# A second attention layer with its steps in another order, and weight halves made by converting and accumulating transfers

## The chip, the cores and the metric

The kernel runs on one core of a Trainium2 chip. Five engines run their own instruction queues: TensorE (PE, with its weight loads shown apart as PEld), VectorE (DVE), ScalarE (ACT), GpSimd (POOL) and SyncE (SP), which here only issues transfers. The metric is the time of one execution on the device in microseconds, as the median of several runs.

## The reference

A trunk of four residual layers over 256 tokens of width 1024 in float32, and a last RMSNorm. Layers 0 and 3 mix tokens with NSA attention, layer 1 with MoBA attention, layer 2 with a gated convolution; a SwiGLU feed-forward part (FFN) follows in each. The change works in layer 1:

```python
q, k, v = jnp.split(h @ w_in, 3, axis=-1)          # 16 heads of 64
n_blk = -(-S_ // MOBA_BLOCK)                       # 256 tokens are one block
...
n_sel = min(MOBA_TOPK, n_blk - 1)                  # 0: no past block to select
...
m_own = jnp.broadcast_to(own_pos[None, :] <= tq[:, None], (B_, H, Qc, MOBA_BLOCK))
s_own = jnp.einsum('bhqd,bhkd->bhqk', qc, k_own)
if n_sel == 0:
    p = masked_softmax(s_own, m_own)
    return jnp.einsum('bhqk,bhkd->bhqd', p.astype(v_own.dtype), v_own)
...
return o @ w_out
```

With 256 tokens and blocks of 256 this is causal attention of 16 heads, between two projections.

## The kernel before

**Weights.** A float32 product is made of three products of float32r halves, high×high, high×low and low×high. All weights come from one stream of 402 *parts* of 128x1024 float32 (512 KB), `in_w`. `load_part` (L115, SP) brings a part into a `raw` tile, `split_part` rounds it to `whi` (L176, `HI` names the engine) and takes `wlo` = raw − whi (L180, `LO` names the engine: "v" is DVE, "p" POOL in four pieces). `take` hands a part to the matmuls and makes `split_part` run for the next ones, so that five are under way. The pools hold six `raw`, five `whi` and five `wlo` tiles. `split_part` already has a branch for the letter "d" in `LO`; no table uses it before. In it a POOL transfer converts the part straight into a `raw` tile that serves as the high half, ACT writes its negative into `wlo`, and a second POOL transfer from the same place in memory is accumulated onto `wlo`. Nothing is left for DVE then, and that `raw` tile stays taken until PE has used it.

**The layer.** `MOBA_ORDER` lists its steps. V projects four parts for half of the values (L602 to L604, 128x512 matmuls); k and q project one part for one pair of heads, 24 matmuls of 128x256 (L206 to L208, with `at` as the other operand; DVE takes the result out of PSUM in L589); s makes a pair's scores (L692 to L694), then `softmax`: a masked reduction on DVE (L619), four exponentials on ACT (L622), a reciprocal `rc` on DVE (L624), and four multiplications of `pr` by it (L626, by the letters of `MOBA_BY`, POOL before). T transposes a pair's `pr` on PE (L704 to L707), P multiplies with the values (L206 to L208 with `pt`). The out projection (`moba_out`, L226 and L230) starts in between. There are eight pairs, 32 parts (103 to 134 of the stream, the last eight `moba_out`). In the FFN before it, POOL also sums squares (`ssq`, L293), and `rstd` (L307) follows at the layer's start.

A scheduler puts the instructions of each engine in a queue of their own by its estimate; waits between engines are semaphores. An engine's queue is taken strictly in order, POOL's transfers among its other instructions.

Of the kernel before, what the change touches and what calls it, by code (L numbers as in the profile page):

```python
# [9 lines left out]
F32 = mybir.dt.float32  # L10
F32R = mybir.dt.float32r
AF = mybir.ActivationFunctionType
OP = mybir.AluOpType
# [3 lines left out]
P = 128  # L17
D = 1024
S = 256
KT = D // P  # L20
NT = S // P
DFF = 2816
FT = DFF // P
DH = 64
# [3 lines left out]
PART = 8  # L28
# [8 lines left out]
ROW_BUFS = 7  # L37
PT_BUFS = 5
PS_BUFS = {"A": 4, "B": 3, "C": 1}
NSA_ORDER = ("A G q K0 F q F K2 F F g E q C K1 q q s q c s t T V D s K3 T q P s T P s q T T s P c P s T t P s "  # L40
             "P T T P P").split()
MOBA_ORDER = ("V k k q q k s V s T q q k s s P k T k q T P q P T P s q q T k s k T s s T P P T P P").split()
LO = {"nsa_out": "p", "moba_out": "vp", "A": "p", "F": "v"}
HI = {"moba_out": "v", "moba_q": "ava"}
OUT_BANKS = "AAAB"
CMP_BANK = "B"
GELU = "vector"
# [5 lines left out]
RUN = 2 * PART  # L53
LAG = 4
PROJ_BANKS = "AABB"
NSA_BY = ["p"] * 8
MOBA_BY = ["p"] * 8
OWN = "vava"
CONE = "vector"
NPAIR = 8  # L60
NCMP = 15
# [3 lines left out]
class Kernel:  # L65
    def __init__(self, ctx, tc, ap):
        self.tc, self.nc, self.ap = tc, tc.nc, ap
        self.operands = ctx.enter_context(tc.tile_pool(name="operands", bufs=2))
        self.const = ctx.enter_context(tc.tile_pool(name="const", bufs=1))
        self.wp = ctx.enter_context(tc.tile_pool(name="wp", bufs=3))  # L70
        self.work = ctx.enter_context(tc.tile_pool(name="work", bufs=2))
        self.ps = ctx.enter_context(tc.tile_pool(name="ps", bufs=2, space=PSUM))
        self.pos = 0
        self.raw = {}
        self.parts = {}
        self.jobs = []
        self.latest = []
        self.nblk = ap["w"].shape[0]
        self.names = [step for step, name, _, c in stream()
                      for _ in range(len(c) // P * (FT if name == "ffn_w_down" else 4 if step == "F" else KT))][::PART]  # L80
        self.seq, q = [], 0
        while q < self.nblk:
            if self.names[q] == "fast":
                self.seq += [(q, w) for w in FAST] + [(q + x, None) for x in range(4, KT)]
                q += KT
            else:
                self.seq.append((q, None))
                q += 1
        self.when = [0]
        for _, what in self.seq:  # L90
            self.when.append(self.when[-1] + (1 if what else 2))
        self.n = 0
# [54 lines left out]
    def split_part(self, x):  # L147
        nc = self.nc
        q, what = self.seq[x]
        if what:  # L150
            self.fast_part(x)
            return
        lo_eng, hi_eng = (e.get(self.names[q], d) for e, d in ((LO, "v"), (HI, "a")))
        lo_eng, hi_eng = (e[q % len(e)] if q >= 4 else d for e, d in ((lo_eng, "v"), (hi_eng, "a")))
        if lo_eng == "d":
            hi = self.wp.tile([P, PART * P], F32R, tag="raw", name=f"raw{q}", bufs=RAW_BUFS)
            lo = self.operands.tile([P, PART * P], F32R, tag="wlo", name=f"wlo{q}", bufs=W_BUFS)
            nc.gpsimd.dma_start(hi, self.ap["w"][q])
            nc.scalar.activation(lo, hi.bitcast(F32), AF.Identity, scale=-1.0)
            nc.gpsimd.dma_start(lo, self.ap["w"][q], accum_op=OP.add)  # L160
            self.parts[x] = (hi, lo)
            return
        if q not in self.raw:
            self.load_part(q)
        src = self.raw.pop(q)
        hi = self.operands.tile([P, PART * P], F32R, tag="whi", name=f"whi{q}", bufs=W_BUFS)
        lo = self.operands.tile([P, PART * P], F32R, tag="wlo", name=f"wlo{q}", bufs=W_BUFS)
        eng = {"p": nc.gpsimd, "v": nc.vector}[lo_eng]
        copy = {"a": nc.scalar.copy, "v": nc.vector.tensor_copy, "d": None}[hi_eng]
        n = PART * P // (2 if q < 4 else 1)  # L170
        if hi_eng == "d":
            nc.gpsimd.dma_start(hi, self.ap["w"][q])
        for o in range(0, PART * P, n):
            c = slice(o, o + n)
            if copy:
                copy(hi[:, c], src[:, c])  # L176
            m = n // (PIECES if eng is nc.gpsimd else 1)
            for b in range(o, o + n, m):
                d = slice(b, b + m)
                eng.tensor_tensor(out=lo[:, d], in0=src[:, d], in1=hi[:, d].bitcast(F32), op=OP.subtract)  # L180
        self.parts[x] = (hi, lo)
# [552 lines left out]


    def nsa(self, j, norm):
        nc, at = self.nc, self.begin(norm)
        mm = nc.tensor.matmul
        self.new_keys()
        w2 = self.sb([P, 2, 2, P], "w2", bufs=1)  # L740
# [8 lines left out]
        for a in range(2):  # L749
            nc.gpsimd.tensor_copy(xs[a][:, :, :, 16], pos[:, a, None, 8:].to_broadcast([P, 4, 8]))  # L750

        def put_raw(a, gp):
            def put(p):
                f = self.scaled(p)
                for i in range(2):
                    src = f[i * DH:(i + 1) * DH].rearrange("p (c r i) -> p i r c", i=2, r=8)
                    dst = xs[a][:, 2 * gp + i, :, :16]
                    nc.vector.tensor_copy(dst[:DH], src[:, 0])
                    nc.scalar.copy(dst[DH:], src[:, 1])
                if gp:  # L760
                    windows(a)
            return put

        def windows(a):
            for hf in range(2):
                for r in range(0, 8, 4):
                    x = self.ff([P, 2, S]).rearrange("p i s -> p (i s)").rearrange("p (r i g c) -> p r i g c", r=4, i=2, g=4)
                    src = xs[a][:, :, r:r + 4, hf:hf + 16].rearrange("p g r c -> p r g c")
                    nc.scalar.copy(x[:, :, 0], src)
                    nc.vector.tensor_tensor(out=x[:, :, 1], in0=src, in1=x[:, :, 0].bitcast(F32), op=OP.subtract)  # L770
                    if hf == 0:
                        src = pos[:, a, r:r + 4, None].to_broadcast([P, 4, 4])
                        nc.scalar.copy(x[:, :, 0, :, 15], src)
                        nc.vector.tensor_tensor(out=x[:, :, 1, :, 15], in0=src, in1=x[:, :, 0, :, 15].bitcast(F32),
                                                op=OP.subtract)
                    xw[a].append(x.rearrange("p r i g c -> p r (i g c)"))
# [103 lines left out]
        def compress_values(_):  # L880
# [4 lines left out]
            for g in range(4):  # L885
                rep = self.row().rearrange("p (i a c) -> p i a c", i=2, c=16)
                c = slice(DH + g * 16, DH + g * 16 + 16)
# [12 lines left out]
            for r in range(4):  # L900
                y = self.ff([P, 4 * P])
                on = self.rsel[:, r:r + 1]
                if OWN[r] == "a":
                    nc.scalar.activation(y, x, AF.Identity, scale=on)
                else:
                    {"v": nc.vector, "p": nc.gpsimd}[OWN[r]].tensor_scalar(y, x, on, None, op0=OP.mult)
                vc.append(y.rearrange("p (g c) -> p g c", g=4))

        ptc = self.sb([P, 4, S], "ptc", F32R, bufs=1)
# [45 lines left out]
        v = [[], []]  # L955
# [16 lines left out]
        def scores(p):  # L972
# [10 lines left out]
            for i in range(2):  # L983
                cols = [(s0[:, i, b], slice(b * P, (b + 1) * P)) for b in range(2)]
                cols += [(s1[i][:, b], slice((1 + b) * S, (2 + b) * S)) for b in range(2)]
                h = 2 * p + i
                g = [gates[:, t, 16 * (b + 1) + h:16 * (b + 1) + h + 1] for t in range(2) for b in range(2)]
                prs[p].append(self.softmax(cols, g, NSA_BY[p]))

        prs, pend, outs = [], [], []  # L990

# [41 lines left out]
        def project_keys(i):  # L1033
            self.project([put_keys(i // 2, i % 2)], at)

        self.steps(NSA_ORDER, {
            "A": project_raw, "K": project_keys, "G": lambda _: self.project([put_gates], at),
            "F": compress, "E": activate, "C": compress_keys, "D": compress_values, "q": project_q,
            "g": turn_gates, "c": compressed, "s": scores,
# [116 lines left out]
def stream():  # L1156

    r = lambda a, n: np.arange(a, a + n)
    out = lambda w, j, step, m=0: ([(step, w, j, r(m * P, 512))]
                                   + [(step, w, j, r(i * P, P)) for i in range(m + 4, KT)])  # L1160
    s = []
    for i in LAYERS:
        j = i // 3
        n = {}
        if i % 3 == 0:
            for step in NSA_ORDER:
                k = step[0]
                n[k] = m = int(step[1:]) if step[1:] else n.get(k, -1) + 1
                cols = {"A": r(1024, 512), "K": r(1536 + m // 2 * 512 + m % 2 * P, P), "G": r(2480, P),
# [28 lines left out]
            s += out("ffn_w_down", i, "down")  # L1198
        else:
            s.append(("down", "ffn_w_down", i, r(0, D)))  # L1200
    return s


def tiles(x):

    x = dict(x)
# [3 lines left out]
    x["ffn_w_down"] = x["ffn_w_down"][:, np.concatenate(rows)]  # L1210
    x["nsa_cmp_w1"] = np.concatenate([x["nsa_cmp_k_w1"], x["nsa_cmp_v_w1"]], axis=2)
    ts = []
    for step, name, j, c in stream():
        w = x[name][j]
        t = wide_tiles(w[c], np.arange(512)) if step == "F" else wide_tiles(w, c)
        if step == "fast":
            b = t[:4 * KT].reshape(2, 2, 2, 4, P, P)
            t = np.concatenate([x.reshape(KT, P, P) for x in (b[0, :, 0], b[0, :, 1], b[1, :, 1], b[1, :, 0])]
                               + [t[4 * KT:]])
        ts.append(t)  # L1220
# [45 lines left out]
```

## Time and profile before

| | us |
|---|---|
| median of 3 runs (lowest, highest) | 1231.16 (1228.86, 1232.27) |
| profiled execution, time | 1231.72 |
| profiled execution, span from first to last instruction | 1229.9 |
| PE busy in the span | 1202.0 |
| DVE, ACT, POOL busy | 985.2, 732.5, 288.0 |
| layer 1's attention on PE (first L602 to about the last L230) | 334.1 to 440.3 |

The span and the end of the execution are 1.8 us apart. A matmul's own duration (0.28 us for 128x256) is longer than the distance of its start from the next one's, since PE works on several at once; what PE loses is read from the distances of starts.

### The profile page before, as it was taken

To read this page: it belongs to the slowest core of one execution; us is meant where nothing else is said; L and a number is where in the kernel's file an instruction comes from. 1 tells how busy PE (TensorE), PEld (TensorE's weight loads), DVE (VectorE), ACT (ScalarE), POOL (GpSimd) and SP (SyncE) were. 2 spreads that over 40 slices of the span, in tenths; PEclk is the share of its full clock that TensorE was granted. 3 is DMA by queue.
4 is the path that set the end of the run, shared out by engine and by line. 5 is a ranking of instruction groups with operands and counts; after the bars stand their busy time and mean duration, and the time that the engine had idled before them with its cause. 6 is when DMAs were issued, how large, how long until landed. Compare 5 with 4: busy or idle time off the path is not lost.

```text
span 1229.9 us, 19380 instructions
## 1 busy us (share of the span) xinstructions
PE 1202.0 (98%) x6628; PEld 1043.2 (85%) x6628; DVE 985.2 (80%) x1743; ACT 732.5 (60%) x1300; POOL 288.0 (23%) x406
## 2 busy tenths in 40 slices
PE   7999999999999999999999999999999989999997
PEld 7988888888899888888888888888899878888886
DVE  7989788886778797887769797896759897889753
ACT  6789656564456535764444555574457896566543
POOL 1068640000111542000113260000230786400000
PEclk9899999999999999999999999999999999999999
DMA  8673265657654545666765655565647632655670
GB/s 313 221 235 88 85 225 165 211 183 252 193 172 154 167 136 175 240 202 194 278 197 164 191 183 175 200 237 164 244 155 244 207 115 74 208 177 198 200 266 35
DMA packets 96451, 231.40 MB, mean 188 GB/s; under 512 B 18272, under 2 KB 43232, under 8 KB 96352
## 3 DMA queue, kind: packets, MB, share of 16 engines
q1 hardware_dynamic: 95920, 229.61, 57.1%
q8 instruction: 52, 0.85, 0.3%
q10 hardware_dynamic: 432, 0.56, 0.1%
q14 instruction: 47, 0.39, 0.1%
HBM read 213.33 MB, written 1.05 MB: 174 GB/s over the span
## 4 chain that ended last, share of the span: by engine, by line
PE 83%; ACT 6%; DVE 5%; issue 2%; DMA 2%; POOL 1%; SPq 0%; POOLq 0%; ACTq 0%; DVEq 0%
PE psA L226 13%; PE psA L230 7%; PE psA L504 5%; PE psA L502 5%; PE psA L503 5%; PE psB L502 4%; PE psB L504 4%; PE psB L503 4%; ACT pr L622 3%; PE psA L208 2%; PE psA L206 2%; PE psA L207 2%; PE psB L226 2%; DVE wlo L180 2%; PE psB L444 1%
## 5 line engine op out<-in xcount | busy, mean ns | idle before, releaser
L176 ACT CAST whi<-raw 128x1024 fp32r<-128x1024 f32 (+1 forms) x363 | 373.3, 1039 | 289.6 <-DMA raw<-in_w 55.8
L180 DVE TENSOR_TENSOR wlo<-raw,whi 128x1024 fp32r<-128x1024 f32 (+1 forms) x350 | 428.3, 1241 | 130.1 <-ACT whi L176 106.4
L226 PE MATMUL psA<-ff,whi 128*128 128x512 f32 x686 | 181.8, 392 | 0.2 <-DVE row L1059 0.2
L226 PEld LDWEIGHTS psA<-ff,whi 128*128 128x128 f32 x686 | 124.8, 189 | 22.8 <-DVE row L1059 0.6
L626 POOL TENSOR_SCALAR pr<-pr,rc,gates 128x256 f32<-128x256 f32 (+1 forms) x128 | 76.9, 614 | 111.3 <-DVE rc L624 109.4
L206 PE MATMUL psA<-at,whi 128*128 128x256 f32 x352 | 101.3, 288 | 0.6 <-ACT whi L176 0.3
L208 PE MATMUL psA<-at,wlo 128*128 128x256 f32 x352 | 100.5, 286 | 1.1 <-DVE wlo L180 1.1
L230 PE MATMUL psA<-ff,wlo 128*128 128x256 f32 x686 | 101.0, 283 | 0.0
L230 PEld LDWEIGHTS psA<-ff,wlo 128*128 128x128 f32 x686 | 96.0, 191 | 5.3
L207 PE MATMUL psA<-at,whi 128*128 128x256 f32 x352 | 100.3, 285 | 0.0
L504 PE MATMUL psA<-whi,at 128*128 128x512 f32 x256 | 99.7, 389 | 0.0
L502 PE MATMUL psA<-whi,at 128*128 128x512 f32 x256 | 99.6, 389 | 0.0
L503 PE MATMUL psA<-wlo,at 128*128 128x512 f32 x256 | 99.6, 389 | 0.0
L136 ACT CAST shi<-B 128x1024 fp32r<-128x1024 f32 x56 | 58.9, 1051 | 54.2 <-DVE B L122 21.0
L293 POOL TENSOR_TENSOR ssq<-ssq,row 128x256 f32<-128x256 f32 x42 | 36.3, 864 | 207.9 <-ACT row L291 150.7
L180 POOL TENSOR_TENSOR wlo<-raw,whi 128x256 fp32r<-128x256 f32 x96 | 70.4, 767 | 34.7 <-issue 17.4
L137 DVE TENSOR_TENSOR slo<-B,shi 128x1024 fp32r<-128x1024 f32 x56 | 66.7, 1216 | 12.0 <-ACT shi L136 12.0
L502 PE MATMUL psB<-whi,at 128*128 128x512 f32 x192 | 75.2, 392 | 0.0
L504 PE MATMUL psB<-whi,at 128*128 128x512 f32 x192 | 74.8, 390 | 0.0
L503 PE MATMUL psB<-wlo,at 128*128 128x512 f32 x192 | 74.7, 389 | 0.0
L622 ACT ACTIVATE pr<-pr,mn 128x128 f32<-128x128 f32 (+1 forms) x160 | 71.2, 448 | 2.4 <-DVE mn L619 1.7
L206 PEld LDWEIGHTS psA<-at,whi 128*128 128x128 f32 x352 | 68.0, 193 | 1.9 <-DVE row L589 0.7
(293 smaller groups left out, 2688.4 us busy)
## 6 DMA issues: line engine op xcount, KB each, us to landing
raw<-in_w SPq DMA_DIRECT2D x368, 512.0 KB, 4.5
B<-in_w SPq DMA_DIRECT2D x32, 512.0 KB, 4.4
pt<-pt SPq DMA_DIRECT2D x320, 32.0 KB, 1.9
ff<-row SPq DMA_DIRECT2D x32, 64.0 KB, 3.4
keys<-keys SPq DMA_DIRECT2D x16, 128.0 KB, 2.9
h<-in_xt SPq DMA_DIRECT2D x4, 256.0 KB, 4.4
raw<-in_w SPq DMA_DIRECT2D x4, 256.0 KB, 4.7
pt<-pt SPq DMA_DIRECT2D x64, 16.0 KB, 3.1
```

What stands on the lines that cost most here:

```text
L176: copy(hi[:, c], src[:, c])
L180: eng.tensor_tensor(out=lo[:, d], in0=src[:, d], in1=hi[:, d].bitcast(F32), op=OP.subtract)
L206: mm(out, wt[0], act[0], start=first, stop=False)
L207: mm(out, wt[0], act[1], start=False, stop=False)
L208: mm(out, wt[1], act[0], start=False, stop=last)
L226: mm(outs[o], w[0], acts[k].rearrange("p i s -> p (i s)"), start=(k == 0), stop=(k == n - 1))
L230: mm(outs[o][:, :S], w[1], acts[k][:, 0, :], start=False, stop=False)
L502: mm(o, a[:, 0, s], hi, start=(k == 0), stop=False)
L503: mm(o, a[:, 0, s], lo, start=False, stop=False)
L504: mm(o, a[:, 1, s], hi, start=False, stop=(k == KT - 1))
L622: nc.scalar.activation(pr[:, c], pr[:, c], AF.Exp, bias=mn[:, j:j + 1], scale=-1.0, accum_out=den[:, j:j + 1])
L626: {"p": nc.gpsimd, "v": nc.vector}[by[j % len(by)]].tensor_scalar(pr[:, c], pr[:, c], rc[:, j:j + 1], gates[j], op0=OP.mult, op1=OP.mult)
```

## The change

The order of the steps is another, the normalisation of pairs 0, 2, 6 and 7 goes from POOL to DVE, and `LO` and `HI` become tables by layer. In the built program sixteen parts take the "d" branch (its description in a few words says thirteen): all eight of `moba_q` (in place of halves by ACT, DVE, ACT in turn and by DVE), every third by number of `moba_k` and every second of `moba_V`. The eight `moba_out` parts get the high half from ACT in place of DVE. The tables of the NSA layers get another form with the same contents.

```diff
-MOBA_ORDER = ("V k k q q k s V s T q q k s s P k T k q T P q P T P s q q T k s k T s s T P P T P P").split()
-LO = {"nsa_out": "p", "moba_out": "vp", "A": "p", "F": "v"}
-HI = {"moba_out": "v", "moba_q": "ava"}
+MOBA_ORDER = ("k k q k q s s T k q q T V k P s V T P q k s q P s T s k T P q k q P T s s T P T P P").split()
+LO = (
...
+    {"moba_out": "vp", "moba_q": "d", "moba_k": "vdv", "moba_V": "vd"},
...
+HI = ({}, {"moba_out": "a"}, {}, {})
...
-MOBA_BY = ["p"] * 8
+MOBA_BY = "vpvpppvv"
...
-        lo_eng, hi_eng = (e.get(self.names[q], d) for e, d in ((LO, "v"), (HI, "a")))
-        lo_eng, hi_eng = (e[q % len(e)] if q >= 4 else d for e, d in ((lo_eng, "v"), (hi_eng, "a")))
+        lo_eng, hi_eng = (e[self.layer[q]].get(self.names[q], d) for e, d in ((LO, "v"), (HI, "a")))
+        n = self.names[:q].count("F") if self.names[q] == "F" else q
+        lo_eng, hi_eng = (e[n % len(e)] if q >= 4 else d for e, d in ((lo_eng, "v"), (hi_eng, "a")))
```

The branch that the sixteen parts now take stands in both kernels, and the tile names there carry other numbers in the two programs:

```python
        if lo_eng == "d":
            hi = self.wp.tile([P, PART * P], F32R, tag="raw", name=f"raw{q}", bufs=RAW_BUFS)
            lo = self.operands.tile([P, PART * P], F32R, tag="wlo", name=f"wlo{q}", bufs=W_BUFS)
            nc.gpsimd.dma_start(hi, self.ap["w"][q])
            nc.scalar.activation(lo, hi.bitcast(F32), AF.Identity, scale=-1.0)
            nc.gpsimd.dma_start(lo, self.ap["w"][q], accum_op=OP.add)
```

Lines of the kernel after stand 11 further down from here on (L626 is L637, L180 is L191, L704 is L715), and the two transfers are its L169 and L171.

**POOL, start of the layer.** Before, the queue goes from the sums of squares over `rstd` to the normalisations of pairs 0 to 2:

```order
L293 TENSOR_TENSOR ssq_3610<-ssq_3610,row_3840 128x256
L307 TENSOR_TENSOR rstd_3987<-var_3985,mhalf 128x2
L626 TENSOR_SCALAR pr_4197<-pr_4197,rc_4200 128x128 x2
L626 TENSOR_SCALAR pr_4197<-pr_4197,rc_4200 128x256 x2
L626 TENSOR_SCALAR pr_4308<-pr_4308,rc_4311 128x128 x2
```

After, where `raw` names a converting and `wlo` an accumulating transfer:

```order
L304 TENSOR_TENSOR ssq_3610<-ssq_3610,row_3839 128x256
L171 DMA wlo_3844<-in_w 128x1024
L171 DMA wlo_3877<-in_w 128x1024
L171 DMA wlo_3907<-in_w 128x1024
L318 TENSOR_TENSOR rstd_3940<-var_3938,mhalf 128x2
L169 DMA raw_4026<-in_w 128x1024
L169 DMA raw_4063<-in_w 128x1024
L171 DMA wlo_3993<-in_w 128x1024
L171 DMA wlo_4027<-in_w 128x1024
L169 DMA raw_4199<-in_w 128x1024
L171 DMA wlo_4064<-in_w 128x1024
L169 DMA raw_4282<-in_w 128x1024
```

`rstd` stands behind accumulating transfers, and each of those behind the ACT instruction that fills its `wlo`.

**POOL, the middle of the layer.** After, the normalisation of pair 3 (`pr_4628`) stands behind the last transfers, and pair 4's (`pr_4700`) behind POOL's share of a `moba_out` part:

```order
L169 DMA raw_4647<-in_w 128x1024
L171 DMA wlo_4551<-in_w 128x1024
L171 DMA wlo_4648<-in_w 128x1024
L637 TENSOR_SCALAR pr_4628<-pr_4628,rc_4631 128x128 x2
L637 TENSOR_SCALAR pr_4628<-pr_4628,rc_4631 128x256 x2
L191 TENSOR_TENSOR wlo_4760<-raw_4757,whi_4759 128x256 x4
L637 TENSOR_SCALAR pr_4700<-pr_4700,rc_4703 128x128 x2
```

A normalisation there now starts once both accumulating transfers have been issued.

**PE, pair 5.** Before, the transposes of pair 5 (`pr_4896`) stand within the scores of pairs 6 and 7:

```order
L208 MATMUL psA_4913<-at_3902,wlo_4665 128x256
L692 MATMUL psA_4964<-keys_3303,ff_4759 128x256
L693 MATMUL psA_4964<-keys_3303,ff_4759 128x256
L694 MATMUL psA_4964<-keys_3303,ff_4759 128x256
L692 MATMUL psA_4968<-keys_3303,ff_4759 128x512
L704 MATMUL psB_4950<-ident,pr_4896 128x128
L693 MATMUL psA_4968<-keys_3303,ff_4759 128x512
L706 MATMUL psB_4950<-ident,pr_4896 128x128
L707 MATMUL psB_4951<-ident,pr_4896 128x128
```

After, pair 5 (`pr_4739`) is transposed behind a q part (`raw_4647`, `wlo_4648`) and the multiplication of pair 4 with the values:

```order
L218 MATMUL psA_4899<-at_3899,raw_4647 128x256
L219 MATMUL psA_4899<-at_3899,wlo_4648 128x256
L217 MATMUL psC_4934<-pt_4804,ff_4510 128x512
L218 MATMUL psC_4934<-pt_4804,ff_4510 128x512
L219 MATMUL psC_4934<-pt_4804,ff_4510 128x512
L217 MATMUL psC_4934<-pt_4805,ff_4516 128x2x128
L715 MATMUL psB_4946<-ident,pr_4739 128x128
L717 MATMUL psB_4946<-ident,pr_4739 128x128
L718 MATMUL psB_4947<-ident,pr_4739 128x128
```

Its scores are about 115 matmuls back there.

**DVE, pair 0.** After, the reciprocal of pair 0 (`rc_4107`) and its normalisation stand behind the last reduction of pair 1 and a whole low half of a k part:

```order
L630 ISA pr_4129,mn_4130<-psA_4125,mask 128x256
L630 ISA mn_4130 128x1
L191 TENSOR_TENSOR wlo_4164<-raw_4161,whi_4163 128x1024
L635 RECIPROCAL rc_4107<-den_4106 128x4
L637 TENSOR_SCALAR pr_4104<-pr_4104,rc_4107 128x128 x2
L637 TENSOR_SCALAR pr_4104<-pr_4104,rc_4107 128x256 x2
```

PE reaches that pair's first transpose 25 matmuls behind pair 1's last score.

More of the change, by code (lines that the diff above doesn't have):

```diff
@@ L39 @@
 PS_BUFS = {"A": 4, "B": 3, "C": 1}
-NSA_ORDER = ("A G q K0 F q F K2 F F g E q C K1 q q s q c s t T V D s K3 T q P s T P s q T T s P c P s T t P s "
-             "P T T P P").split()
-MOBA_ORDER = ("V k k q q k s V s T q q k s s P k T k q T P q P T P s q q T k s k T s s T P P T P P").split()
-LO = {"nsa_out": "p", "moba_out": "vp", "A": "p", "F": "v"}
-HI = {"moba_out": "v", "moba_q": "ava"}
+NSA_PLAN = (
+    {"order": ("A G q K0 F q F K2 F F g E q C K1 q q s q c s t T V D s K3 T q P s T P s q T T s P c P s "
+               "T t P s P T T P P").split(),
+     "pairs": ("va", "va", "va", "va"), "windows": ("vvvv", "vvvv"), "by": "pppppppp", "own": "vava"},
+    {"order": ("A G q K0 F q F K2 F F g E q C K1 q q s q c s t T V D s K3 T q P s T P s q T T s P c P s "
+               "T t P s P T T P P").split(),
+     "pairs": ("va", "va", "va", "va"), "windows": ("vvvv", "vvvv"), "by": "pppppppp", "own": "vava"},
+)
+MOBA_ORDER = ("k k q k q s s T k q q T V k P s V T P q k s q P s T s k T P q k q P T s s T P T P P").split()
+LO = (
+    {"nsa_out": "p", "A": "p"},
+    {"moba_out": "vp", "moba_q": "d", "moba_k": "vdv", "moba_V": "vd"},
+    {},
+    {"nsa_out": "p", "A": "p"},
+)
+HI = ({}, {"moba_out": "a"}, {}, {})
 OUT_BANKS = "AAAB"
@@ L55 @@
 PROJ_BANKS = "AABB"
-NSA_BY = ["p"] * 8
-MOBA_BY = ["p"] * 8
-OWN = "vava"
+MOBA_BY = "vpvpppvv"
 CONE = "vector"
@@ L78, in __init__ @@
         self.nblk = ap["w"].shape[0]
-        self.names = [step for step, name, _, c in stream()
-                      for _ in range(len(c) // P * (FT if name == "ffn_w_down" else 4 if step == "F" else KT))][::PART]
+        parts = [(step, i) for step, name, i, _, c in stream()
+                 for _ in range(len(c) // P * (FT if name == "ffn_w_down" else 4 if step == "F" else KT))][::PART]
+        self.names, self.layer = zip(*parts)
         self.seq, q = [], 0
@@ L736, in nsa @@
     def nsa(self, j, norm):
-        nc, at = self.nc, self.begin(norm)
+        nc, at, plan = self.nc, self.begin(norm), NSA_PLAN[j]
         mm = nc.tensor.matmul
@@ L750, in nsa @@
             nc.gpsimd.tensor_copy(xs[a][:, :, :, 16], pos[:, a, None, 8:].to_broadcast([P, 4, 8]))
+        copy_by = {"v": nc.vector.tensor_copy, "p": nc.gpsimd.tensor_copy, "a": nc.scalar.copy}
         def put_raw(a, gp):
@@ L757, in put @@
                     dst = xs[a][:, 2 * gp + i, :, :16]
-                    nc.vector.tensor_copy(dst[:DH], src[:, 0])
-                    nc.scalar.copy(dst[DH:], src[:, 1])
+                    for b, by in enumerate(plan["pairs"][2 * a + gp]):
+                        copy_by[by](dst[b * DH:(b + 1) * DH], src[:, b])
                 if gp:
@@ L764, in windows @@
         def windows(a):
+            lows = iter({"v": nc.vector, "p": nc.gpsimd}[by] for by in plan["windows"][a])
             for hf in range(2):
@@ L769, in windows @@
                     nc.scalar.copy(x[:, :, 0], src)
-                    nc.vector.tensor_tensor(out=x[:, :, 1], in0=src, in1=x[:, :, 0].bitcast(F32), op=OP.subtract)
+                    by = next(lows)
+                    by.tensor_tensor(out=x[:, :, 1], in0=src, in1=x[:, :, 0].bitcast(F32), op=OP.subtract)
                     if hf == 0:
@@ L902, in compress_values @@
                 on = self.rsel[:, r:r + 1]
-                if OWN[r] == "a":
+                if plan["own"][r] == "a":
                     nc.scalar.activation(y, x, AF.Identity, scale=on)
                 else:
-                    {"v": nc.vector, "p": nc.gpsimd}[OWN[r]].tensor_scalar(y, x, on, None, op0=OP.mult)
+                    {"v": nc.vector, "p": nc.gpsimd}[plan["own"][r]].tensor_scalar(y, x, on, None, op0=OP.mult)
                 vc.append(y.rearrange("p (g c) -> p g c", g=4))
@@ L987, in scores @@
                 g = [gates[:, t, 16 * (b + 1) + h:16 * (b + 1) + h + 1] for t in range(2) for b in range(2)]
-                prs[p].append(self.softmax(cols, g, NSA_BY[p]))
+                prs[p].append(self.softmax(cols, g, plan["by"][p]))
         prs, pend, outs = [], [], []
@@ L1034, in project_keys @@
             self.project([put_keys(i // 2, i % 2)], at)
-        self.steps(NSA_ORDER, {
+        self.steps(plan["order"], {
             "A": project_raw, "K": project_keys, "G": lambda _: self.project([put_gates], at),
@@ L1159, in stream @@
     out = lambda w, j, step, m=0: ([(step, w, j, r(m * P, 512))]
-                                   + [(step, w, j, r(i * P, P)) for i in range(m + 4, KT)])
-    s = []
+                                   + [(step, w, j, r(n * P, P)) for n in range(m + 4, KT)])
+    parts = []
     for i in LAYERS:
+        s = []
         j = i // 3
@@ L1165, in stream @@
         if i % 3 == 0:
-            for step in NSA_ORDER:
+            for step in NSA_PLAN[j]["order"]:
                 k = step[0]
@@ L1200, in stream @@
             s.append(("down", "ffn_w_down", i, r(0, D)))
-    return s
+        parts += [(step, name, i, j, c) for step, name, j, c in s]
+    return parts
 def tiles(x):
@@ L1212, in tiles @@
     ts = []
-    for step, name, j, c in stream():
+    for step, name, _, j, c in stream():
         w = x[name][j]
```

## The prediction

> **What bounds the kernel now.** I read the page first: the busy lines, then the chain that ended last.
>
> ```profile
> span 1229.9 us, 19380 instructions
> PE 1202.0 (98%) x6628; PEld 1043.2 (85%) x6628; DVE 985.2 (80%) x1743; ACT 732.5 (60%) x1300; POOL 288.0 (23%) x406
> PE 83%; ACT 6%; DVE 5%; issue 2%; DMA 2%; POOL 1%; SPq 0%; POOLq 0%; ACTq 0%; DVEq 0%
> ```
>
> PE is the bound, busy in 98% of the span; work taken off DVE or POOL is worth only the PE waits that it ends. The change works in layer 1's attention, so next come the windows of that stage (columns: length, then busy time of PE, PEld, DVE, ACT, POOL with instruction counts, granted clock, DMA share, GB/s).
>
> ```profile
> 350.00:360.00 10.00, 10.00 (x85) 10.00 (x84) 8.56 (x14) 5.37 (x9) 0.00 (x0) 1.00 0.65 201
> 410.00:420.00 10.00, 8.86 (x68) 7.98 (x66) 9.13 (x27) 5.26 (x17) 4.90 (x8) 1.00 0.60 180
> 420.00:430.00 10.00, 9.70 (x56) 7.86 (x55) 6.30 (x23) 6.74 (x23) 6.21 (x13) 1.00 0.53 188
> 334.10:440.30 106.20, 104.67 (x699) 95.01 (x698) 84.98 (x198) 59.42 (x148) 27.86 (x49) 1.00 0.50 161
> ```
>
> PE's idle time by this count is 1.5 us in 106.2, nearly all of it between 410 and 430. Waits shorter than a matmul's run don't show there, so I add up what the stage's matmuls take at the spacing of undisturbed starts.
>
> ```profile
> L206 PE MATMUL psA<-at,whi 128*128 128x256 f32 x128 | 36.5, 285 | 0.0
> L602 PE MATMUL psA<-whi,at 128*128 128x512 f32 x32 | 12.6, 393 | 0.0
> L226 PE MATMUL psA<-ff,whi 128*128 128x512 f32 x29 | 8.4, 399 | 0.0
> L692 PE MATMUL psA<-keys,ff 128*128 128x512 f32 x8 | 3.2, 396 | 0.0
> ...
> 334.13 0.40 PE L602 MATMUL psA<-whi,at 128*128 128x512 f32 x1
> 335.28 0.39 PE L604 MATMUL psA<-whi,at 128*128 128x512 f32 x1
> ...
> 414.25 0.28 PE L206 MATMUL psA<-at,whi 128*128 128x256 f32 x1
> 417.11 0.28 PE L692 MATMUL psA<-keys,ff 128*128 128x256 f32 x1
> ```
>
> Between the first two starts lie five spacings, 0.230 each; between the last two the 24 matmuls of one q part, 0.119 each and 2.86 us in all. The stage has 181 matmuls of 512 columns (three lines of 32 for the values, 37 of the out projection, 24 of scores, 24 of weighing), 464 of 256 columns (three lines of 128, 32, 24, 24), and 50 small ones at an estimated 0.11: 41.6 + 55.2 + 5.5 = 102.3 us. So at most 106.2 − 102.3 = 3.9 us (0.32%) can be won in the stage, and what counts as different from no change here is 0.3%, 3.7 us. Outside this stage the change alters no work.
>
> Where the larger part of it goes, PE's own timeline shows:
>
> ```profile
> 417.47 0.39 PE L692 MATMUL psA<-keys,ff 128*128 128x512 f32 x1
> 418.53 0.33 PE L704 MATMUL psB<-ident,pr 128*128 128x128 f32 x1 [0.67 <-POOL pr L626]
> 418.62 0.48 PE L693 MATMUL psA<-keys,ff 128*128 128x512 f32 x1
> 419.57 0.33 PE L706 MATMUL psB<-ident,pr 128*128 128x128 f32 x1 [0.47 <-POOL pr L626]
> 419.85 0.27 PE L704 MATMUL psB<-ident,pr 128*128 128x128 f32 x1
> 420.19 0.33 PE L706 MATMUL psB<-ident,pr 128*128 128x128 f32 x1
> ...
> 425.20 0.48 PE L226 MATMUL psA<-ff,whi 128*128 128x512 f32 x1
> 425.91 0.33 PE L706 MATMUL psB<-ident,pr 128*128 128x128 f32 x1 [0.24 <-POOL pr L626]
> ```
>
> Start to start against an undisturbed 0.23 or 0.11: 417.47 loses 0.83, 418.62 0.72, 419.85 0.23, together 1.8 us for pair 5; 425.20 loses 0.48 for pair 6. The other 1.6 us lie in pieces of about 0.2 and less. Behind pair 5's wait stand DVE and POOL:
>
> ```profile
> 416.70 1.22 DVE L180 TENSOR_TENSOR wlo<-raw,whi 128x1024 fp32r<-128x1024 f32 x1
> 417.83 0.17 DVE L624 RECIPROCAL rc<-den 128x4 f32<-128x4 f32 x1
> 418.11 2.03 POOL L626 TENSOR_SCALAR pr<-pr,rc 128x128 f32<-128x128 f32 x4 [4.36 <-DVE rc L624]
> ```
>
> POOL stood idle for 4.36 us until DVE's reciprocal, which stood behind a low half in DVE's queue.
>
> **The change part by part.**
>
> ```profile
> L180 DVE TENSOR_TENSOR wlo<-raw,whi 128x1024 fp32r<-128x1024 f32 x24 | 29.6, 1235 | 7.3 <-ACT whi L176 6.7 <-PE psB L230 0.2
> L176 DVE CAST whi<-raw 128x1024 fp32r<-128x1024 f32 x11 | 9.2, 835 | 2.3 <-PE psA L207 1.3 <-issue 0.4 <-PE psA L604 0.4
> L176 ACT CAST whi<-raw 128x1024 fp32r<-128x1024 f32 x18 | 18.8, 1047 | 23.3 <-PE psA L604 6.3 <-issue 4.5 <-PE psA L207 3.6
> L619 DVE CUSTOM_DVE_ANT_0 pr<-psA,mask 128x256 f32<-128x256 f32 x16 | 6.3, 419 | 0.3 <-PE psA L694 0.2
> L626 POOL TENSOR_SCALAR pr<-pr,rc 128x256 f32<-128x256 f32 x16 | 9.6, 612 | 0.0
> L626 POOL TENSOR_SCALAR pr<-pr,rc 128x128 f32<-128x128 f32 x16 | 5.7, 372 | 46.2 <-DVE rc L624 46.2
> ```
>
> *Removed from DVE:* 16 low halves x 1.235 = 19.8 us and 11 casts, 9.2 us; *added to it:* 16 normalisations, between 0 and POOL's 0.61 each, so at most 8 x 0.61 + 8 x 0.37 = 7.9 us. DVE goes from 85 to 56–64 us of the stage. *ACT:* 16 negations at the cast's 1.05 us replace the casts of 13 of those parts, and eight `moba_out` casts come in: 3 + 8 = 11 more, 11.5 us, to 71 of 106. Neither is the bound; these totals are worth nothing in themselves, only through order. *SP* issues 16 loads fewer, which no engine feels.
>
> *Pair 5.* Its scores now lie about 115 matmuls, some 14 us, ahead of its transposes, against 28 before; the chain from scores to normalised `pr` fits in that. Gain 1.8 us (if it fails, none: the end 0).
>
> *Pairs 6 and 7* are still transposed soon after their scores, behind pair 7's scores (6 matmuls, 1.05 us), six of weighing (1.05) and eight of 512 (1.85): 4.0 us. Before, the two chains ended with
>
> ```profile
> 420.38 0.48 PE L694 MATMUL psA<-keys,ff 128*128 128x512 f32 x1
> ...
> 424.69 1.62 POOL L626 TENSOR_SCALAR pr<-pr,rc 128x128 f32<-128x128 f32 x4 [1.04 <-DVE rc L624]
> 426.50 1.62 POOL L626 TENSOR_SCALAR pr<-pr,rc 128x128 f32<-128x128 f32 x4 [0.19 <-DVE rc L624]
> ```
>
> (first the last score matmul of pair 6, then the normalisations of pairs 6 and 7) for pair 6 at 426.31, 5.5 us after its scores' end at 420.86. On DVE the four multiplications cost less than 1.62, so I take 5.0: 1.0 us of wait, against 0.48. Loss 0.5 (0 to 1.5).
>
> *Pair 0.* Behind pair 1's last score, PE has 24 matmuls of a k part, 2.9 us. DVE has two reductions of 0.42, the 1.24 of the low half set ahead, 0.17 for `rc`, and the normalisation: 0.8 + 1.2 + 0.2 + up to 1.6, so 2.2 to 3.8, its middle 0.1 over the 2.9; a DVE that still works off pair 1's reductions adds some half a microsecond. Loss 0.7 (0 to 1.5).
>
> *Pair 3* waits on POOL for the accumulating transfer of a part further on, which needs PE to have used an older `wlo`. It has slack but not much: loss 0.2 (0 to 1). The small pieces I leave as they are.
>
> *The 32 POOL transfers.* The trace of before has none issued by POOL, so their time is bounded by SP's of the same 512 KB:
>
> ```profile
> DMA to landing us min/median/max: 3.3/4.5/8.3
> raw<-in_w SPq DMA_DIRECT2D x23, 512.0 KB, 3.6
> q1 hardware_dynamic: 3798, 13.83, 47.9%
> ```
>
> (first all of SP's weight loads of the program; then those of 345 to 435 us and the queue's share of the 16 engines there). Between issue and need a part has this much: its low half can't be accumulated before PE frees the `wlo` of the part five back; then ACT writes the negative, 1.05 us; then four parts of 2.86 us go by on PE, 11.4, so the transfer has 10.4 us. The nearest rows are 3.6 and 4.5, the longest 8.3, and an accumulating transfer that reads and writes its target may take twice a plain one: 9.0 at the median, 16.6 at the worst. I take 7, which is hidden. The converting transfers have 7 to 13 us, for the `raw` tile is now held until PE is done; 4.5 fits, 8.3 does not everywhere. Sixteen more readings of 512 KB raise the share of the transfer engines in the stage by some half of 48%, to 70 to 95%: busy, not full. Cost 0, ends 0 and (16.6 − 10.4) x 5 = 31 us, once per five parts for 24 parts.
>
> The Trainium skill, "DMA: Bandwidth & Descriptors", section "Anatomy of one DMA — SWDGE (gpsimd) path", gives 2.0 us plus bytes over 436e3, an estimate of 3.2 us for 512 KB; by it the term is 0 as well.
>
> *POOL's queue.* An issue on it is priced by nothing here; between 0 and about the duration of a POOL instruction (0.6). 32 x 0.6 = 19 us beside an engine with 28 us of work in 106: hidden, unless an issue that waits for ACT holds up `rstd` or a normalisation. Taken as 0 (to 3 us, if pair 1's and pair 3's normalisation come 1.5 us late each).
>
> *Sum:* −1.8 + 0.5 + 0.7 + 0.2 = −0.4 us, so 1231.7 becomes 1231.3 for the profiled execution, which stood 0.6 above the median of 1231.16; as a median 1230.8 us.
>
> **The rivals.**
>
> *A, accumulation late (the other side).* If a transfer from POOL takes longer than 10.4 us from issue to landing, PE waits at each round of five parts: at 12 us 5 x 1.6 = 8 us, 1239; it passes 0.3% from 11.2 us on. For it: reading and writing the target, twice the longest plain load, and DMA shares of 0.60 already. Against it: the median of 4.5 and the share of 48%. A second way to it: if POOL could prepare a transfer only while DVE leaves it alone, then with DVE 8.56 busy of 10 a preparation as long as one pair's normalisation, 1.62, would stretch to 1.62 / 0.144 = 11 us, and 11 + 4.5 − 10.4 = 5 us five times is +25, at 1256; with DVE at 60% of the stage the same 1.62 become 4, 8.5 in all, which is hidden. So that way decides only where DVE stays as full as before, and I give it 3 of A's 17 in 100. That is the rule of the Trainium skill, "SBUF — State Buffer", in its warning "DVE blocks DMA": the descriptors of POOL's transfers can't be written while DVE runs a 2-port operation, to which its float32 copies belong. No run here shows it yet.
>
> *B, all is recovered.* No pair waits, no small piece: −3.9, 1227.3. For it: DVE loses a quarter or more of its work and ACT stays under 70%. Against it: pairs 6 and 7 still follow their scores closely.
>
> *C, POOL's queue holds.* The transfers' issues, each waiting for ACT's negation, hold `rstd` or the normalisations of pairs 1, 3 and 4. POOL was idle ahead of the first of them for long:
>
> ```profile
> 365.52 2.69 POOL L626 TENSOR_SCALAR pr<-pr,rc 128x128 f32<-128x128 f32 x4 [19.80 <-DVE rc L624]
> ```
>
> so there is room; the price is 1.5 us for each held pair, +3 to +5: 1234 to 1236.
>
> *D, nothing moves.* The transfers are hidden, and the new order's waits equal the old ones: 1231.2; I count it with the forecast.
>
> **How the numbers follow.** Forecast with D: 0.58, own range 1228.5 to 1233. B: 0.14. A: 0.17. C: 0.11, of which a good half ends past 1234.9. Faster than 1227.5 is then 0.14 (all of B), slower 0.17 + 0.07 = 0.24, same 0.62. The range of 8 in 10 takes all of B and C and the light half of A: 1227.2 to 1239.
>
> **What would show it.** Right: the first matmul of each "d" part starts without a wait for its `wlo`; POOL's transfers land in 3.5 to 9 us; no wait at pair 5's transposes; 0.5 to 1.5 us at pairs 6 and 7 and about 0.7 at pair 0, now released by DVE; the stage lasts 105.8 us. Wrong: PE waiting at L219 for a transfer into `wlo` (A), at the transposes for POOL (C), or a stage of under 103 us (B). A gain or loss outside 334 to 440 us would mean that I missed a coupling.

## The result: 0.6% slower

| | before | after |
|---|---|---|
| median of six runs, us | 1231.67 | 1238.47 |
| lowest to highest, us | 1228.86 to 1232.27 | 1236.14 to 1239.78 |

The ratio is 1.0061, 95% interval 1.0051 to 1.0071. The prediction was 1230.8, no change. The measured time lies near the upper end of its wide range, 1227.2 to 1239, outside the 1228.5 to 1233 of the forecast itself, and on the slow side, where a small gain had been expected.

The page after, span, busy engines, and the transfer queues (q1 is SP's, q0 POOL's; packets, MB, share of the 16 transfer engines):

```profile
span 1238.0 us, 19400 instructions
PE 1203.5 (97%) x6628; PEld 1043.3 (84%) x6628; DVE 963.5 (78%) x1732; ACT 742.9 (60%) x1311; POOL 304.4 (25%) x422
q1 hardware_dynamic: 93616, 221.22, 54.9%
q0 software_dynamic: 4608, 16.78, 5.9%
```

PE does the same work in 8.1 us more. DVE has 21.7 us less work, and it bought nothing. The stage's windows (columns as in the prediction):

```profile
334.10:440.30 106.20, 100.06 (x665) 90.46 (x664) 63.36 (x183) 66.14 (x154) 35.99 (x56) 0.98 0.87 234
350.00:360.00 10.00, 7.50 (x61) 7.26 (x61) 6.39 (x28) 8.73 (x25) 2.80 (x6) 1.00 1.05 256
390.00:400.00 10.00, 8.61 (x67) 8.05 (x65) 1.58 (x5) 3.00 (x7) 2.75 (x4) 1.00 0.97 237
400.00:410.00 10.00, 8.15 (x46) 7.14 (x45) 7.29 (x25) 8.23 (x20) 2.70 (x6) 0.83 0.93 253
```

PE stands idle where it did not before, and the last column but one says more: the transfer engines are at 0.87 on average (0.50 before) and at 1 in places (it adds up what all packets took, so that it can pass 1 where packets overlap). PE's own rows at these places:

```profile
349.70 0.40 PE L705 MATMUL psA<-keys,ff 128*128 128x512 f32 x1
352.60 0.62 PE L703 MATMUL psA<-keys,ff 128*128 128x256 f32 x2 [2.50 <-ACT ff L276]
...
397.89 0.28 PE L219 MATMUL psA<-at,wlo 128*128 128x256 f32 x1
399.56 0.35 PE L703 MATMUL psA<-keys,ff 128*128 128x256 f32 x1 [1.40 <-DVE ff L682]
399.76 0.28 PE L704 MATMUL psA<-keys,ff 128*128 128x256 f32 x1
399.87 0.28 PE L705 MATMUL psA<-keys,ff 128*128 128x256 f32 x1
402.00 0.74 PE L703 MATMUL psA<-keys,ff 128*128 128x512 f32 x1 [1.85 <-DVE ff L682]
```

Start against start, PE loses 2.7, 1.6 and 2.0 us there. It waits for no weight: it waits for `ff`, which ACT, and DVE behind it, make. At 352.60 these are the halves of the q that the scores read. At 399.56 and 402.00 they are halves of the values (L682), which the scores don't read; by the program what the scores need there is the PSUM tile, `psA`, that this work empties. ACT's rows, and two of POOL's:

```profile
351.19 1.04 ACT L187 CAST whi<-raw 128x1024 fp32r<-128x1024 f32 x1 [2.24 <-DMA raw<-in_w]
352.14 0.40 ACT L276 CAST ff<-row 128x256 fp32r<-128x256 f32 x1
...
385.60 1.05 ACT L187 CAST whi<-raw 128x1024 fp32r<-128x1024 f32 x1 [3.88 <-DMA raw<-in_w]
...
397.47 1.06 ACT L170 ACTIVATE wlo<-raw 128x1024 fp32r<-128x1024 f32 x1 [6.82 <-DMA raw<-in_w]
398.44 0.82 ACT L681 ACTIVATE ff<-psA,rstd 128x256 fp32r<-128x256 f32 x2
```

```profile
389.00 0.88 POOL L171 DMA_DIRECT2D wlo<-in_w  x1 [8.91 <-ACT wlo L170]
389.60 0.83 POOL L169 DMA_DIRECT2D raw<-in_w  x1
```

ACT stands in order on a load by SP that is late; the `ff` of the next pair is the row behind. At 385.60 the same again, so the accumulating transfer that needs ACT's negation is late, the converting transfer queued behind it on POOL is issued at 389.60 and takes 7.8 us to landing, and ACT stands 6.82 us on that one with the values' `ff` behind it. After the last wait the granted clock was at half for 3.4 us, some 1.7 us more:

```profile
402.00:405.40 3.40, 3.40 (x13) 3.11 (x14) 3.23 (x9) 2.12 (x4) 0.56 (x1) 0.50 0.80 155
```

And the transfers themselves, from 320 to 440 us:

```profile
q0 software_dynamic: 4319, 15.72, 57.3%
q1 hardware_dynamic: 3191, 11.63, 28.4%
...
raw<-in_w SPq DMA_DIRECT2D x19, 512.0 KB, 5.0
wlo<-in_w POOLq DMA_DIRECT2D x16, 512.0 KB, 7.5
raw<-in_w POOLq DMA_DIRECT2D x13, 512.0 KB, 6.4
```

SP's plain loads, 3.7 at the median and 5.8 at the longest in these 120 us before, take 5.0 and up to 8.6.

For what follows I use one more number: PE's lost time from 320 to 460 us, the sum over its matmuls of the distance to the next start less the undisturbed distance. It is 3.9 us before and 9.7 after; the three waits and the halved clock are some 8 of these 9.7. The other 2 us of the 8.1 lie in layer 3, whose program is the same and whose waits differ from execution to execution (a halved clock at 945 us here, one at 938 in a run without any POOL transfer, none before); I don't put them down to the change.

### The profile page after: what moved, and what is told of

It reads as the page before. It is cut to its first block, busy times and chain, and to the rows that moved or that the text cites. A ratio compares the mean times of both kernels' runs of the same rounds, so it can differ in the third digit from the quotient of the medians.

```text
span 1238.0 us, 19400 instructions
## 1 busy us (share of the span) xinstructions
PE 1203.5 (97%) x6628; PEld 1043.3 (84%) x6628; DVE 963.5 (78%) x1732; ACT 742.9 (60%) x1311; POOL 304.4 (25%) x422
## 3 DMA queue, kind: packets, MB, share of 16 engines
HBM read 221.72 MB, written 1.05 MB: 180 GB/s over the span
## 5 line engine op out<-in xcount | busy, mean ns | idle before, releaser
L187 ACT CAST whi<-raw 128x1024 fp32r<-128x1024 f32 (+1 forms) x358 | 368.2, 1040 | 273.8 <-DMA raw<-in_w 68.7
L191 DVE TENSOR_TENSOR wlo<-raw,whi 128x1024 fp32r<-128x1024 f32 (+1 forms) x334 | 408.5, 1241 | 127.6 <-ACT whi L187 98.6
L637 POOL TENSOR_SCALAR pr<-pr,rc,gates 128x256 f32<-128x256 f32 (+1 forms) x128 | 77.3, 618 | 112.9 <-DVE rc L635 111.0
L191 POOL TENSOR_TENSOR wlo<-raw,whi 128x256 fp32r<-128x256 f32 x96 | 70.2, 766 | 30.2 <-ACT whi L187 13.9
L217 PE MATMUL psA<-at,whi 128*128 128x256 f32 x256 | 74.3, 291 | 2.6 <-ACT whi L187 2.5
L218 PE MATMUL psA<-at,whi 128*128 128x256 f32 x256 | 73.7, 288 | 0.0
L219 PEld LDWEIGHTS psA<-at,wlo 128*128 128x128 f32 x352 | 68.6, 195 | 1.9 <-DVE wlo L191 1.9
```

Of the source, the lines that this page charges most:

```text
L217: mm(out, wt[0], act[0], start=first, stop=False)
L218: mm(out, wt[0], act[1], start=False, stop=False)
L219: mm(out, wt[1], act[0], start=False, stop=last)
L637: {"p": nc.gpsimd, "v": nc.vector}[by[j % len(by)]].tensor_scalar(pr[:, c], pr[:, c], rc[:, j:j + 1], gates[j], op0=OP.mult, op1=OP.mult)
```

## The experiments

Two theories to begin with. S, slots: a part made by POOL transfers keeps its `raw` tile until PE is done with it, so later loads are issued late. T, transfers: the POOL transfers keep the transfer engines busy, so loads land late. Rivals were the order itself (O) and, later, POOL's queue (Q). All ratios are against the kernel before on the same chip; the runs were spread over several chips, so rows are compared by their ratios rather than by their medians.

The last column is the transfer engines' share from 320 to 440 us.

| run | what is different from the kernel after | median, us | ratio (95%) | PE lost, us | engines' share |
|---|---|---|---|---|---|
| after | – | 1238.47 | 1.0061 (1.0051–1.0071) | 9.7 | 0.86 |
| e1 | tables of halves of before | 1230.81 | 1.0007 (0.9998–1.0015) | 3.3 | 0.52 |
| e2 | order and normalisation of before | 1235.43 | 1.0044 (1.0032–1.0056) | 7.9 | 0.80 |
| e3 | seven raw tiles, 25 ff tiles | 1241.61 | 1.0103 (1.0087–1.0119) | 11.8 | 0.84 |
| e4 | 25 ff tiles | 1236.95 | 1.0062 (1.0050–1.0074) | 11.0 | 0.86 |
| e10 | no accumulating transfers | 1229.04 | 0.9988 (0.9977–0.9999) | 1.3 | 0.55 |
| e13 | negations on POOL | 1247.09 | 1.0136 (1.0119–1.0153) | 21.5 | 0.84 |
| e6 | eight q parts only | 1229.29 | 0.9992 (0.9982–1.0002) | 2.1 | 0.72 |
| e7 | casts of the plain parts on DVE | 1236.28 | 1.0049 (1.0031–1.0066) | 8.6 | 0.86 |
| e15 | accumulating 128 of 1024 columns | 1229.19 | 0.9989 (0.9980–0.9998) | 1.2 | 0.63 |
| e16 | second transfer without accumulation | 1229.34 | 0.9996 (0.9985–1.0007) | 2.0 | 0.74 |
| e9 | eight k and V parts only | 1232.05 | 1.0014 (1.0005–1.0022) | 5.4 | 0.70 |
| e19 | five q parts only | 1228.69 | 0.9990 (0.9981–1.0000) | 1.8 | 0.67 |
| e18 | none by POOL transfers | 1230.06 | 1.0001 (0.9992–1.0010) | 2.8 | 0.52 |

**Order or halves.** The change cut in two.

```diff
-    {"moba_out": "vp", "moba_q": "d", "moba_k": "vdv", "moba_V": "vd"},
+    {"moba_out": "vp"},
...
-HI = ({}, {"moba_out": "a"}, {}, {})
+HI = ({}, {"moba_out": "v", "moba_q": "ava"}, {}, {})
```

> The kernel after with the tables of halves of before (no part by POOL transfers, q and out high halves as before); the new order of steps and the new normalisation table stay. Theory S (slots): the parts made by POOL transfers keep their raw tile until PE has used it, so later loads are issued late, ACT's queue stands in order on one of them and the halves of a q behind it come late. By S the loss goes with those parts: 1230 to 1232.5, and the waits of 2.7, 1.6 and 2.0 us at the scores are gone. Rival O (order): the new order sets the scores too close behind their q; by O 1236 or more, with the waits at the scores still there. Rival T (transfers): POOL's transfers are simply slow (6.4 and 7.5 us) on transfer engines that are full; by T 1230 to 1232.5 as well.

Measured 1230.81, no difference from before. In the other half the order and the normalisation go back:

```diff
-MOBA_ORDER = ("k k q k q s s T k q q T V k P s V T P q k s q P s T s k T P q k q P T s s T P T P P").split()
+MOBA_ORDER = ("V k k q q k s V s T q q k s s P k T k q T P q P T P s q q T k s k T s s T P P T P P").split()
...
-MOBA_BY = "vpvpppvv"
+MOBA_BY = "pppppppp"
```

> The new tables of halves with the order of steps and the normalisation (all on POOL) of before. Part numbers fall otherwise on the steps in that order, so thirteen parts are made by POOL transfers instead of sixteen. By S slower than before too, 1234 to 1240, with ACT standing on a raw tile that lands late, ahead of PE waiting at scores or at an L217 line. By O the same as before, 1230 to 1232.5. By T slower, 1234 to 1240, with PE waiting for wlo itself or the shares of the transfer engines near 1.

Measured 1235.43: the loss goes with the halves, O falls. With this order thirteen parts take the "d" branch, since the table goes by part numbers, which is where "thirteen" comes from.

**One more raw tile,** and its control, since the room has to come from somewhere.

```diff
-RAW_BUFS = 6
+RAW_BUFS = 7
...
-FF_BUFS = 26
+FF_BUFS = 25
```

> The kernel after with seven raw tiles instead of six, and 25 instead of 26 ff tiles to pay for the room. By S each load and conversion can be issued one part (2.86 us) sooner; ACT's waits of 2.2, 3.9 and 6.8 us shrink by up to that each and the waits at the scores by most of it: 2 to 5 us faster than the run with 25 ff tiles alone. By O and by T the same as that run within 1 us.

> Control: the kernel after with 25 ff tiles and six raw tiles. All theories: within 1.5 us of the kernel after, 1237 to 1240.

The control is as the kernel after; the seventh tile makes it slower still, by 4.7 us. S as I had put it falls: with room for loads to go earlier, ACT stands on them no less than before (19.8 us in all from 320 to 440 us, 16.2 in the control). T had put this run within 1 us of its control, so it missed too.

```profile
383.17 1.04 ACT L187 CAST whi<-raw 128x1024 fp32r<-128x1024 f32 x1 [4.36 <-DMA raw<-in_w]
```

(The schedule differs too in that run, so its 4.7 us aren't a price of the tile alone, and what they come from stays open. The trace is of its fastest execution, 1238.81.)

**Without the accumulating transfers.** Tiles held as long as before, negations and converting transfers kept.

```diff
-            nc.gpsimd.dma_start(lo, self.ap["w"][q], accum_op=OP.add)
```

> The kernel after without its sixteen accumulating transfers; it leaves out the addition of the weights to the low halves, so that those hold the negative of the high half alone. The raw tiles are held as long as before, the negations and the converting transfers stay. Theory S (raw tiles held, loads issued late): the waits stay, 1235 to 1239. Theory T (accumulating transfers keep the transfer engines busy, so that plain loads which took 3.5 us land after 7 to 8): 1229 to 1232, plain loads back at 3.5 to 4.5 us, the engines' share in the stage under 0.75.

Measured 1229.04, PE loses 1.3 us. The transfers from 320 to 440 us there:

```profile
q1 hardware_dynamic: 3600, 13.11, 34.0%
q0 software_dynamic: 2049, 7.42, 20.8%
...
raw<-in_w SPq DMA_DIRECT2D x21, 512.0 KB, 3.7
raw<-in_w POOLq DMA_DIRECT2D x13, 512.0 KB, 4.0
```

One load shows it best: the one that ACT waited for at 351.19 in the kernel after. It is held up by its tile alike in both, issued at 343.4 and 343.6, and here is its time to landing, in the kernel after:

```profile
DMA to landing us min/median/max: 7.8/7.8/7.8
```

and without accumulation:

```profile
DMA to landing us min/median/max: 3.4/3.4/3.4
```

Without accumulation the load's own packets (q1) are on the engines in the second microsecond behind its issue. In the kernel after POOL's queue alone is there (first its line, then that without accumulation), and the load's first packet starts 3.5 us behind the issue:

```profile
q0 software_dynamic: 85, 0.29, 124.8%
...
q1 hardware_dynamic: 47, 0.19, 84.4%
```

**Accumulation, bytes, or the queue?** Leaving the transfers out also frees POOL's queue and saves bytes. Two runs keep the order of the queues as it is. In one the accumulating transfer is an eighth as large:

```diff
-            nc.gpsimd.dma_start(lo, self.ap["w"][q], accum_op=OP.add)
+            nc.gpsimd.dma_start(lo[:, :P], self.ap["w"][q][:, :P], accum_op=OP.add)
```

> The kernel after with accumulating transfers of 128 of the 1024 columns; it leaves out the addition to the other 896 columns of the low halves. The queues of all engines stand as in the kernel after, each accumulating transfer still waits for ACT's negation in POOL's queue. Theory T (the time of the accumulating transfers on the engines): 1228.5 to 1231. Rival Q (POOL's queue stands on ACT's negations and holds the converting transfers behind): 1235 to 1239, as the kernel after.

1229.19: POOL's instructions still wait for ACT in the same order, and each second transfer still takes 0.87 us of POOL, so Q falls. In the other it is as large, but doesn't accumulate:

```diff
-            nc.gpsimd.dma_start(lo, self.ap["w"][q], accum_op=OP.add)
+            nc.gpsimd.dma_start(lo, self.ap["w"][q])
```

> The kernel after with the second transfer of each part converting onto the low half's tile instead of accumulating; it leaves out the subtraction, the low halves hold the weights. Same bytes from memory, same queues in the same order. If what costs is the reading and writing of the target that accumulation adds: 1229 to 1232.5, the engines' share near 0.75. If it is the second 512 KB by itself: 1234 to 1239.

1229.34. The same bytes from memory in the same order cost nothing that can be told from no change; accumulating them costs about 8 us (ratios of 1.0061 and 0.9996). Its transfers from 320 to 440 us, then POOL's queue over the whole program, here and without the second transfers (e10):

```profile
q0 software_dynamic: 4243, 15.42, 41.4%
...
wlo<-in_w POOLq DMA_DIRECT2D x16, 512.0 KB, 4.7
...
q0 software_dynamic: 4608, 16.78, 4.4%
...
q0 software_dynamic: 2304, 8.39, 2.3%
```

The sixteen second transfers take 4.4 − 2.3 = 2.1 points of the engines' time there, the sixteen accumulating ones 5.9 − 2.3 = 3.6. By this estimate, which gives the converting transfers the same 2.3 points in all three runs, accumulating takes about 1.7 times as much, some 2.8 against 1.6 us of all 16 engines each (0.036 x 1238 / 16 and 0.021 x 1226 / 16). Why it takes more, no run shows.

**Who waits for the late loads.** In the trace ACT was the link; two runs move its work.

```diff
-HI = ({}, {"moba_out": "a"}, {}, {})
+HI = ({}, {"moba_out": "a", "moba_k": "v", "moba_V": "v"}, {}, {})
```

> The kernel after with the casts of the eight k and V parts that are still loaded by SP on DVE instead of ACT. If ACT's stand on a late plain load is the link to PE, the wait of 2.7 us at 350 goes and ACT reaches its negations sooner, so the later ones shrink: 1231 to 1235. If DVE merely stands there in its place, and with it the other half of the same q: 1236 to 1240.

1236.28, with 3.5 us lost at 350, so that wait stays. Now DVE stands on the load, with the row that ACT needs behind it:

```profile
351.37 0.69 DVE L187 CAST whi<-raw 128x1024 fp32r<-128x1024 f32 x1 [3.05 <-DMA raw<-in_w]
...
352.87 0.42 DVE L600 TENSOR_TENSOR row<-psA,rb 128x256 f32<-128x256 f32 x1
...
353.33 0.40 ACT L276 CAST ff<-row 128x256 fp32r<-128x256 f32 x1 [4.10 <-DVE row L600]
```

PE's waits that came from ACT's stand at 385 and 397 are gone there. The other moves the negations:

```diff
-            nc.scalar.activation(lo, hi.bitcast(F32), AF.Identity, scale=-1.0)
+            nc.gpsimd.tensor_scalar(lo, hi.bitcast(F32), -1.0, None, op0=OP.mult)
```

> The kernel after with the sixteen negations on POOL instead of ACT. ACT then no longer stands on converting transfers, only on plain loads. If ACT's stand on a converted tile (6.8 us ahead of 397 us) is the link to PE, the waits of 1.6 and 2.0 us at the scores there go and with them the halved clock behind them: 1232 to 1235, the wait at 350 us stays. If the transfers are late whatever engine waits for them, 1237 or more, with PE waiting for wlo or POOL's queue (sixteen times some 2.5 us more work) holding the normalisations.

1247.09. This run doesn't answer the question: a negation is 2.96 us on POOL, not some 2.5, and POOL becomes the wait itself, at a normalisation.

```profile
L170 POOL TENSOR_SCALAR wlo<-raw 128x1024 fp32r<-128x1024 f32 x16 | 47.4, 2964 | 16.3 <-DMA raw<-in_w 11.6 <-issue 3.1 <-PE psA L241 1.6
...
419.06 0.48 PE L715 MATMUL psB<-ident,pr 128*128 128x128 f32 x1 [6.90 <-POOL pr L637]
```

**Fewer of them.** Tables `{"moba_out": "vp", ...}` with `"moba_q": "d"` alone; with `"moba_k": "vdv", "moba_V": "vd"` alone; with `"moba_q": "dv"`; and with none of these.

> The kernel after with only the eight q parts made by POOL transfers; k and V parts all by ACT and DVE. Half of the accumulating transfers: by T the share of the engines falls and so do the landings, 1230 to 1233. By S eight tiles are still held, but never two neighbours of them for long: 1231 to 1235. If neither the number nor the tiles matter but the order (shown not to by the run with the order alone), 1238.

> The kernel after with the eight k and V parts of its sixteen made by POOL transfers and the q parts by ACT and DVE. If the loss grows with the number of accumulating transfers in a stretch: about as the run with the eight q parts, 1228.5 to 1232. If the q parts are harmless and the k and V parts are not: 1235 or more.

> The kernel after with POOL transfers for the q parts of even number only (five parts). Share of the transfer engines near before's 0.52 to 0.65; DVE keeps more low halves. By T no loss is left at eight parts, so fewer bring nothing more: within 1 us of the run with eight q parts, 1228.5 to 1230.5.

> The kernel after with no part by POOL transfers, all k, q and V parts cast on ACT and subtracted on DVE; the new order, the new normalisation and the eight out casts on ACT stay. If the microsecond or so by which the runs with eight and five parts beat the kernel before comes from the order, the normalisation and ACT's casts: 1228.5 to 1229.5, as with five parts. If it needs DVE to be relieved by transfers: 1230 to 1231.5, as with the order alone.

Eight q parts cost nothing (1229.29); eight k and V parts do, a little (1.0014), so the number isn't all. There ACT stands 5.78 us on a plain load of a V step that takes four parts at once:

```profile
373.99 1.05 ACT L187 CAST whi<-raw 128x1024 fp32r<-128x1024 f32 x1 [5.78 <-DMA raw<-in_w]
```

Five q parts gave 1228.69, none 1230.06. The intervals of the two ratios touch (0.9981–1.0000 and 0.9992–1.0010), so whether a few transfers gain the tenth of a per cent between them stays open. Beside e10 and e15, which leave work out, none is clearly faster than the kernel before.

## Why the prediction was wrong

- **The step that failed is the term "the 32 POOL transfers", put at 0.** I asked whether each POOL transfer arrives before PE needs it, 10.4 us. They did: I took 7 for an accumulating one, it was 7.5 at the median and 11.0 at the longest, and no matmul waited for a `wlo` that a transfer filled. What I left out is what the accumulating transfers do to the plain loads and the converting transfers beside them. I had the engines at "70 to 95%: busy, not full"; they were at 0.87 with stretches at 1.05, and there SP's loads took 5.0 us at the median and up to 8.6 (3.7 and 5.8 before), the converting transfers 6.4 and up to 12.0 (4.2 and 6.6 without accumulation). These have no 10.4 us: a plain load waits for a held `raw` tile, and its cast, like the negation of a converted tile, stands in ACT's queue ahead of work that PE needs at once. Term as measured: some 9 us (ratios of 1.0061 and of 0.9988 without accumulation), 8.4 of it as PE's lost time in the stage (9.7 against 1.3).
- **Rival A** had the right culprit, the accumulating transfer, and the wrong victim. Its condition, an accumulating transfer that lands later than 11.2 us, was never met (11.0 at the longest, with no wait of PE for it); that its price, 8 us, comes near the measured 9 is luck. A's second way, POOL's preparation held off by DVE, is not needed: with the same queues and 512 KB without accumulation the loss is gone. Whether the rule of the Trainium skill, "SBUF — State Buffer", in its warning "DVE blocks DMA", acts here at all, no run shows.
- **The size from the Trainium skill.** Its "DMA: Bandwidth & Descriptors", section "Anatomy of one DMA — SWDGE (gpsimd) path", gave an estimate of 3.2 us for 512 KB; a converting transfer took 3.7 at least, 4.2 at the median (without accumulation beside it), but an accumulating one 5.2 at least. The formula is near for the first and not for the second.
- **Rival C and POOL's queue:** an issue costs POOL 0.6 (converting) to 0.9 us (accumulating), against 0 to 0.6 assumed; no loss by it (e15). POOL's queue did hand ACT's delay on, to the converting transfer behind, once the loads were late.
- **Pair 5** was right: its 1.8 us are gone in e1, e10 and e18. **Pairs 6 and 7**, put at 1.0 us of wait, lose at most 0.2 at any start in e10 and e18; **pair 0**, put at 0.7, shows no wait in any of them. **Pair 3**, put at 0.2, waits 0.85 in e1 and less than 0.1 at any start in the kernel after. By PE's lost time in the stage the order and the normalisation gain 0.6 us (e1), with ACT's `moba_out` casts 1.1 (e18), and 2.6 where converting transfers relieve DVE as well (e10), against 0.4 foreseen; all too little to be told from no change in the whole.
- **"Thirteen"** was no dispute over what the change does: sixteen in this order, thirteen in the old one.

## What to carry to other kernels

Before a transfer is called hidden, ask not only whether it arrives in time but what it does to the landing of every other transfer of that stretch, and which in-order queue stands on those. An engine that prepares weights and also empties PSUM passes a late load straight to PE. An accumulating transfer is not a second read of the same bytes: here it took about 1.7 times the engine time. Add up the transfer engines' share by stretches of ten microseconds, not only on average. How near 1 is too near these runs don't settle: in the run whose second transfers don't accumulate one stretch at 0.98 (360 to 370 us) cost nothing, while with eight k and V parts two at 1.00 and 0.98 (360 to 380 us) went with a loss of 0.14%.

## What the runs showed of the hardware

An accumulating transfer of 512 KB into SBUF took 5.2 us at least and, by the estimate above, about 1.7 times the engine time of the same transfer without accumulation. A negation of 128x1024 took 2.96 us on POOL against 1.06 on ACT. Of twelve places in these runs where PE lost over 1.5 us between 320 and 460 us, nine went with a granted clock of one half for 3.4 or 6.8 us that began during the wait or within 3 us behind it; there a wait of 2 us cost nearly 4. The 2.7 us at 350 in the kernel after were one of the three that didn't. In the nine runs without such a place, the kernel before among them, the granted clock stayed full in this stretch.
